# Residual additions of a one-layer hybrid encoder moved from GpSimd into accumulating DMAs on a copy of x in DRAM

## The chip, the core and the metric

The kernel runs on one core of a Trainium2 chip. The metric is the device time of one execution in microseconds; lower is better. Everything is fp32: each matrix product is made of three matmuls on a high and a low half (`fp32r`), which keeps fp32 accuracy. The engines' names are those of the profile: PE (TensorE), DVE (VectorE), ACT (ScalarE), POOL (GpSimd), and SP (SyncE), which does nothing here but issue DMAs.

## The reference, cut to what matters

`x_prompt` has 2048 rows and `x_sample` 128 rows (8 x 16) of 1024 columns. In tiles of 128 rows that makes 17 tiles, 0 to 15 for the prompt and 16 for the sample. The layer is

```python
h = rms_norm(x, norm_g[0])
z = h @ w_in                                   # 3592 columns: q, k, v of attention and of the mLSTM, gates
...                                            # chunk-band attention, mLSTM
mix = jnp.concatenate([att, mlstm_out], axis=-1) @ w_out
x = x + rms_norm(mix, norm_g[1])
ffn, new_buf = conv_ffn(rms_norm(x, norm_g[2]), conv_buf, w_up, w_conv, b_conv, w_down)
x = x + rms_norm(ffn, norm_g[3])
```

The change concerns the two lines `x = x + rms_norm(...)`.

## The kernel before, in words

The kernel is one function, `hymba_step`, with many nested helpers and generators. The source gives instructions and their data dependences; the order in which each engine's queue holds them is set when the program is built, by a scheduler that estimates when each instruction could start (`schedule_with_timeline_sim=True`). Only where the source says `tc.keep_in_program_order` does an instruction stay where it was written. At run time each engine works through its queue strictly in order, and an instruction that must wait holds up all that stand behind it. That is so for DMAs as well: SP and POOL issue them in the order of their queues, and an issue that has to wait (for a buffer, for data) blocks the later ones.

The stages, in order of time:

1. **Projection w_in and mixing** (0 to about 1050 us). The rows of x are loaded tile by tile (`xr`, L224), normed (square on ACT L228, `rsqrt` on POOL L87 and L93, scaling on DVE L231), transposed on PE (`hT_pt`, L76), and split into high and low halves (ACT L210, DVE L211). With these, PE works through 14 groups of 256 columns of w_in, `va0` first (`va`, L104 to L106), then `qk0`. The weights of a group come in two loads into a single raw buffer (`wi_raw`, L1213), so the second load is issued only when the first has been split by ACT L1219 and DVE L1220. In `va0` the nine tiles 0 to 7 and 16 are normed while PE uses the first of them; tiles 1, 4, 7 and 16 share one buffer for their rows, tiles 2 and 5 another, tiles 0, 3 and 6 two more, so the load of tile 4 waits for the transposes of tile 1, that of tile 7 for those of tile 4, that of tile 16 for those of tile 7. Attention and the mLSTM run between the groups.
2. **Projection w_out** (about 1050 to 1330 us; `project`, L974 on). Per tile t: the mixed rows `mr` are normed, transposed and split (`mt`), PE multiplies them by w_out in two halves (`wo`), DVE copies the result into the first 1024 columns of a buffer `mx` (L1026), its squares are summed, and DVE scales it by the norm (L1038). The second 1024 columns of `mx` are named `xr`: SP loads x into them at the start of the tile (L1016), POOL adds the two (L1039), SP stores the sum to `x2d[t]` in DRAM (L1040). `mx` has two buffers of the tag `wl`, which the weights of the next stage (`wul`, L1310) take over at the end.
3. **ConvFFN in three blocks** of 6, 6 and 5 tiles (about 1330 to 2776 us). Each block has an up stage (22 steps f, with `conv` per step: POOL copies two columns between `halo` and the tiles `uu`, `ug`, L1494 and L1499, and DVE L1503 and L1504 need them) and a down stage. The block's rows come from `x2d` (`x2r`, L1079). The result of a block's down stage goes to DRAM (`f0d`, `f1d`), and is finished during the up stage of the next block, in the generators `later` and `delayed`: per tile and half, SP loads the half `v` and the half `x` of `x2d[t]` (L1427, L1428), DVE scales `v` by the norm (L1431), POOL adds `x` (L1432) and issues the store to the output (L1433). There are 24 such units, 12 in block 1 and 12 in block 2. The last block finishes itself at the end (`load_rest`, `finish`), also from `x2d`.

Of the kernel before, what the change touches and what calls it, by code (L numbers as in the profile page):

```python
# [13 lines left out]
ALU = mybir.AluOpType  # L14
# [4 lines left out]
D = 1024  # L19
# [30 lines left out]
def hymba_step(ctx: ExitStack, tc: tile.TileContext, I: dict, O: dict):  # L50
    nc = tc.nc
# [8 lines left out]
    def ps_mm(name):  # L60
        return psum.tile([P, 512], F32, tag="mm", name=name)
# [7 lines left out]
    def spare_tile(name):  # L69
        return spare.tile([P, 512], F32, tag="k", name=name)  # L70

    def dt_(shape, name):
        return dram.tile(shape, F32, tag=name, name=name)
# [12 lines left out]
    def mean_square(ms, ssq, n, eps=EPS):  # L86
        nc.gpsimd.tensor_scalar(ms, ssq, 1.0 / n, eps, op0=ALU.mult, op1=ALU.add)  # L87

    def rsqrt_mean(ssq, n, name, eps=EPS):
        ms = small.tile([P, 1], F32, tag="ms", name=name + "_ms")  # L90
        mean_square(ms, ssq, n, eps)
        rs = small.tile([P, 1], F32, tag="rs", name=name + "_rs")
        nc.gpsimd.tensor_tensor(rs, ms, nhalf[:, 0:1], op=ALU.pow)  # L93
        return rs

    def norm_row(i):
        t = const.tile([P, D], F32, tag="grow", name=f"norm_row{i}")
        nc.sync.dma_start(t, I["norm_g"][i:i + 1, :].broadcast_to([P, D]))
        return t


    def mm3(out, ah, al, bh, bl, start, stop, onto=False):

        nc.tensor.matmul(out, ah, bh, start=start, stop=False, skip_group_check=onto)  # L104
        nc.tensor.matmul(out, ah, bl, start=False, stop=False, skip_group_check=onto)  # L105
        nc.tensor.matmul(out, al, bh, start=False, stop=stop, skip_group_check=onto)  # L106
# [21 lines left out]
    x2d = [dt_([P, D], f"x2d{t}") for t in range(17)]  # L128

    def x_src(t):  # L130
        return I["x_sample"] if t == SAMPLE else I["x_prompt"][t * P:(t + 1) * P, :]
# [69 lines left out]
    def rows_to_T(hrow, chunk, j, name, bank):  # L201
        w = 4 if bank is not ps_big else KT
        for q in range(KT // w):
            pt = bank(f"{name}_pt{q}")
            for k in range(w):
                transpose(pt[:, k * P:(k + 1) * P], hrow[:, (w * q + k) * P:(w * q + k + 1) * P])
            ptv = pt.rearrange("p (k t) -> p k t", k=w)
            hv = chunk[:, 0, w * q:w * q + w, j * P:(j + 1) * P]
            lv = chunk[:, 1, w * q:w * q + w, j * P:(j + 1) * P]
            nc.scalar.copy(hv, ptv)  # L210
            nc.vector.tensor_tensor(lv, ptv, hv, op=ALU.subtract)  # L211
# [4 lines left out]
    def rows_tile(tag, shape, name, dtype=F32):  # L216
        if tag == "xr":
            return rows.tile(shape, dtype, tag="xr", name=name, bufs=2)
        return pa.tile(shape, dtype, tag=tag, name=name, bufs=1)
# [750 lines left out]
    def drain():  # L970
        while any([p_.step() for p_ in pipes]):
            pass

    def project(tiles):  # L974

        ss = [SimpleNamespace(t=t) for t in tiles]

        def load(s):
            t = s.t
            if t == 8:  # L980
                drain()
                open_ffn()
            s.m = rows_tile("xr", [P, D], f"mr{t}")
            if t == SAMPLE:
                for b in range(DB):
                    own = bass.AP(atts[b].tensor, atts[b].offset, [[512, DS], [DS * 512 + DA, HA], [1, DA]])
                    nc.sync.dma_start(s.m[b * DS:(b + 1) * DS, 0:512].rearrange("p (h d) -> p h d", h=HA), own)
                nc.sync.dma_start(s.m[:, 512:D], mixs)
            else:
                nc.sync.dma_start(s.m, mixd[t // 4][:, t % 4, :])  # L990

        def norm(s):
            mt = wpool.tile([P, 2112], F32R, tag="wh", name=f"mt{s.t}", bufs=2)
            ssq = small.tile([P, 1], F32, tag="ssq", name=f"assq{s.t}")
            nc.scalar.activation(mt[:, :512], s.m[:, :512], AF.Square, accum_out=ssq)
            rs = rsqrt_mean(ssq, 512, f"att{s.t}")
            nc.vector.tensor_scalar(s.m[:, :512], s.m[:, :512], rs, None, op0=ALU.mult)
            s.mt = mt[:, :2 * D].rearrange("p (a k n) -> p a k n", a=2, k=KT)

        def turn_rows(s):  # L1000
            rows_to_T(s.m, s.mt, 0, f"mT{s.t}", ps_mm if s.t < 8 else ps_big)

        load(ss[0])
        norm(ss[0])
        yield 0.0, 0.3
        turn_rows(ss[0])
        load(ss[1])
        yield 0.9, 1.2
        for n_, s in enumerate(ss):
            t = s.t  # L1010
            nxt = ss[n_ + 1] if n_ + 1 < len(ss) else None
            if nxt:
                norm(nxt)
            mx = wpool.tile([P, 2112], F32, tag="wl", name=f"mx{t}", bufs=2)
            m, xr = mx[:, 0:D], mx[:, D:2 * D]
            nc.sync.dma_start(xr, x_src(t))  # L1016
            for hf in range(2):
                c = slice(hf * 512, hf * 512 + 512)
                acc = ps_mm(f"wo{t}_{hf}")
                for k in range(KT):  # L1020
                    mm3(acc, s.mt[:, 0, k, :], s.mt[:, 1, k, :], wo[k][0][:, c], wo[k][1][:, c],
                        start=(k == 0), stop=(k == KT - 1))
                    if k % 4 == 3:
                        yield 2.6, 0.5
                ssq = small.tile([P, 1], F32, tag="wssq", name=f"wssq{t}_{hf}")
                nc.vector.tensor_copy(m[:, c], acc)  # L1026
                idle = m[:, 512:D] if hf == 0 else s.mt[:, 0, 0:4, :].rearrange("p k n -> p (k n)")
                nc.scalar.activation(idle, m[:, c], AF.Square, accum_out=ssq)
                if hf == 0:
                    ssa = ssq  # L1030
                    mean_square(ssa, ssq, D)
                    if nxt:
                        turn_rows(nxt)
                        if n_ + 2 < len(ss):
                            load(ss[n_ + 2])
                        yield 0.9, 1.2
            rs = rsqrt_mean(ssq, D, f"n1_{t}", ssa)
            nc.vector.scalar_tensor_tensor(m, m, rs, g1[0], op0=ALU.mult, op1=ALU.mult)  # L1038
            nc.gpsimd.tensor_tensor(xr, m, xr, op=ALU.add)  # L1039
            nc.sync.dma_start(x2d[t], xr)  # L1040

# [5 lines left out]
    def open_ffn():  # L1049

        p1.close()
        ffn.p3 = ctx.enter_context(tc.tile_pool(name="p3", bufs=2, reuse_waits="tile"))
        ffn.halo = ffn.p3.tile([P, 44, 2], F32, tag="halo", name="halo", bufs=1)
        nc.vector.memset(ffn.halo, 0.0)
        ffn.g2 = ffn.p3.tile([P, D], F32, tag="g2", name="g2", bufs=1)
        nc.sync.dma_start(ffn.g2, I["norm_g"][2:3, :].broadcast_to([P, D]))
        pipes[:] = [Pipe(h2_units(0, lead=6)), Pipe(iter([]))]
# [187 lines left out]
    for n_, (half, gi) in enumerate(seq):  # L1245
# [22 lines left out]
        if n_ == len(seq) - 1:  # L1268
            out = project([0, 1, 2, 3, 4, 5, 6, 7, SAMPLE, 8, 9, 10, 11, 12, 13, 14, 15])
            split = w_out_steps()  # L1270
            next(split)
            next(out)
# [128 lines left out]
    def out_rows(t):  # L1401
        return O["y_sample"] if t == SAMPLE else O["y_prompt"][t * P:(t + 1) * P, :]
# [20 lines left out]
    def later(t, rs):  # L1423

        def unit(half):
            v, x, c = spare_tile(f"f{half}{t}"), spare_tile(f"x{half}{t}"), half * 512
            tc.keep_in_program_order(nc.sync.dma_start(v, (f0d, f1d)[half][t]))  # L1427
            tc.keep_in_program_order(nc.sync.dma_start(x, x2d[t][:, c:c + 512]))  # L1428
            yield 0.0, 0.0
            tc.keep_in_program_order(  # L1430
                nc.vector.scalar_tensor_tensor(v, v, rs, g3[:, c:c + 512], op0=ALU.mult, op1=ALU.mult))  # L1431
            nc.gpsimd.tensor_tensor(v, v, x, op=ALU.add)  # L1432
            nc.gpsimd.dma_start(out_rows(t)[:, c:c + 512], v)  # L1433
            yield 0.0, 1.0

        return [unit(half) for half in range(2)]

    def delayed(units):

        for u in units:  # L1440
            next(u)
            yield
            next(u)

    ph.close()
    p4 = ffn.p4 = ctx.enter_context(tc.tile_pool(name="p4", bufs=1, side="right", reuse_waits="tile"))
# [3 lines left out]
    g3 = norm_row(3)  # L1450
# [15 lines left out]
    for b, tiles in enumerate(FBLOCKS):  # L1466
# [124 lines left out]
        for fi, f in enumerate(ORDERS[b]):  # L1591
# [12 lines left out]
            e, c = ec[:, 0:512], ec[:, 512:1024]  # L1604
# [120 lines left out]
        for dh in range(2):  # L1725
# [59 lines left out]
            for j in order:  # L1785
                if dh == 0:
                    half, ssq = out[j]
# [3 lines left out]
                else:  # L1791
                    half, ssq = out[j]
# [3 lines left out]
                    rs = p3.tile([P, 1], F32, tag=f"drs{j}", name=f"drs{tiles[j]}", bufs=2)  # L1796
# [104 lines left out]
```

## Time and profile before

| | |
|---|---|
| median of 3 runs | 2776.57 us (2775.95 to 2780.12) |
| the profiled execution: its own time | 2778.06 us |
| the profiled execution: its span | 2776.4 us, granted PE clock 0.997 |
| busy share of the span: PE, DVE, ACT, POOL | 97%, 70%, 51%, 22% |
| DMA | 522.15 MB, mean 188 GB/s |

A row of the timeline shows start, duration, engine, line, operation, out<-in, shapes, count, and in brackets how long the engine sat idle before it and what ended that. "SPq" and "POOLq" rows of DMA are the issue alone: the transfer lands later, which a waiting engine shows as "<-DMA". Busy shares in the view of stretches are us of each engine in the stretch, the granted clock, the mean busy share of the 16 DMA engines and the GB/s that they moved.

### The profile page before, as it was taken

How to read it: one execution, taken by the hardware profiler on the slowest of the kernel's cores; microseconds unless marked ns; L12 is line 12 of the kernel's file. 1: busy time of each engine (PE TensorE's matmuls, PEld its weight loads, DVE VectorE, ACT ScalarE, POOL GpSimd, SP SyncE). 2: the span in 40 equal slices, each digit the busy share in tenths (PEclk: the TensorE clock that was granted, in tenths of full speed). 3: DMA queues.
4: the chain of work that ended last, by engine and by line, in shares of the span. 5: the costliest groups of instructions: out<-in, count | busy, mean ns of one | idle time of the engine just before them, and what ended most of it. 6: DMA issues, size and time to landing. Idle time of an engine off the chain costs nothing.

```text
span 2776.4 us, 47521 instructions
## 1 busy us (share of the span) xinstructions
PE 2704.6 (97%) x16488; PEld 2530.5 (91%) x16488; DVE 1938.4 (70%) x3563; ACT 1420.4 (51%) x2879; POOL 610.1 (22%) x1177
## 2 busy tenths in 40 slices
PE   8999999999999999999999999999999999999998
PEld 7899999998899998878999998789999778999886
DVE  5344455646546668766999987668998866999744
ACT  4355555634356666543545455445455665555542
POOL 1000010211100002344433322123442102344100
PEclk9999999999999999999999999999999999999999
DMA  5544355556554456345645559866775767776655
GB/s 183 157 118 137 103 164 169 161 151 210 161 182 142 140 165 196 107 166 197 227 157 181 170 192 326 299 223 198 232 220 168 251 218 233 219 238 202 193 184 180
DMA packets 317664, 522.15 MB, mean 188 GB/s; under 512 B 58210, under 2 KB 154302, under 8 KB 317294
## 3 DMA queue, kind: packets, MB, share of 16 engines
q1 hardware_dynamic: 249246, 394.21, 46.3%
q0 software_dynamic: 23248, 79.51, 7.5%
q10 hardware_dynamic: 44928, 45.37, 5.0%
q8 instruction: 130, 2.13, 0.3%
q14 instruction: 112, 0.92, 0.1%
HBM read 377.38 MB, written 144.72 MB: 188 GB/s over the span
## 4 chain that ended last, share of the span: by engine, by line
PE 53%; DVE 3%; issue 2%; DMA 2%; ACT 1%; POOL 1%; DVEq 0%; POOLq 0%; SPq 0%; ACTq 0%
PE uec L104 6%; PE uec L105 6%; PE uec L106 6%; PE dn L106 3%; PE dn L104 3%; PE dn L105 3%; PE ua L106 3%; PE ua L105 3%; PE ua L104 3%; PE dnm L106 2%; PE dnm L105 2%; PE dnm L104 2%; PE wo L106 2%; PE wo L104 2%; PE wo L105 2%
## 5 line engine op out<-in xcount | busy, mean ns | idle before, releaser
L104 PE MATMUL uec<-B,wuh 128*128 128x384 f32 (+1 forms) x720 | 235.4, 328 | 3.2 <-DVE uu L1632 1.7
L105 PE MATMUL uec<-B,wuh 128*128 128x384 f32 (+1 forms) x720 | 235.1, 327 | 0.0
L106 PE MATMUL uec<-B,wul 128*128 128x384 f32 (+1 forms) x720 | 233.5, 327 | 0.0
L1309 ACT CAST wuh<-wu 128x512 fp32r<-128x512 f32 x255 | 141.7, 618 | 114.3 <-PE uec L105 106.3
L1310 DVE TENSOR_TENSOR wul<-wu,wuh 128x512 fp32r<-128x512 f32 x255 | 168.3, 695 | 4.1 <-DMA x2d<-mx 2.9
L405 DVE CUSTOM_DVE_ANT_0 tmp<-s,nb 128x640 f32<-128x640 f32 (+4 forms) x128 | 94.3, 737 | 95.1 <-PE s L395 93.4
L104 PE MATMUL vo<-wi_h,hT 128*128 128x256 f32 x544 | 155.2, 285 | 0.6 <-DVE mt L211 0.6
L106 PE MATMUL vo<-wi_h,hT 128*128 128x256 f32 x544 | 155.6, 286 | 0.0
L105 PE MATMUL vo<-wi_l,hT 128*128 128x256 f32 x544 | 154.8, 285 | 0.0
L1310 DVE TENSOR_TENSOR gl<-gr,gh 128x768 fp32r<-128x768 f32 (+3 forms) x92 | 73.9, 812 | 98.9 <-ACT gh L1309 91.1
L104 PEld LDWEIGHTS uec<-B,wuh 128*128 128x128 f32 x720 | 135.0, 188 | 5.3 <-DVE uu L1632 2.3
L1309 ACT CAST gh<-gr 128x768 fp32r<-128x768 f32 (+3 forms) x92 | 65.0, 719 | 143.8 <-PE dn L105 110.3
L104 PE MATMUL qk<-hT,wi_h 128*128 128x384 f32 (+1 forms) x384 | 129.1, 336 | 7.1 <-ACT qk_st L236 5.3
L105 PEld LDWEIGHTS uec<-B,wuh 128*128 128x128 f32 x720 | 135.2, 188 | 0.2
L106 PEld LDWEIGHTS uec<-B,wul 128*128 128x128 f32 x720 | 135.1, 188 | 0.0
L418 DVE TENSOR_TENSOR ptl<-pt,pth 128x640 fp32r<-128x640 f32 (+4 forms) x128 | 93.6, 737 | 58.4 <-ACT pth L417 57.5
L406 ACT ACTIVATE tmp<-tmp,mn 128x640 f32<-128x640 f32 (+4 forms) x128 | 97.6, 762 | 65.0 <-DVE mn L405 62.4
L105 PE MATMUL qk<-hT,wi_h 128*128 128x384 f32 (+1 forms) x384 | 128.0, 333 | 0.0
L105 PE MATMUL qb<-hT,wi_h 128*128 128x384 f32 (+1 forms) x384 | 127.8, 333 | 0.0
L106 PE MATMUL qk<-hT,wi_l 128*128 128x384 f32 (+1 forms) x384 | 127.5, 332 | 0.0
L106 PE MATMUL qb<-hT,wi_l 128*128 128x384 f32 (+1 forms) x384 | 127.2, 331 | 0.0
L104 PE MATMUL qb<-hT,wi_h 128*128 128x384 f32 (+1 forms) x384 | 127.1, 331 | 0.0
(447 smaller groups left out, 9335.1 us busy)
## 6 DMA issues: line engine op xcount, KB each, us to landing
wu<-in_w_up SPq DMA_DIRECT2D x220, 256.0 KB, 4.3
wu<-wsd SPq DMA_DIRECT2D x176, 256.0 KB, 3.8
wdr<-in_w_down SPq DMA_DIRECT2D x121, 256.0 KB, 5.6
wi_raw<-in_w_in SPq DMA_DIRECT2D x52, 512.0 KB, 4.1
wsd<-ws POOLq DMA_DIRECT2D x88, 256.0 KB, 3.5
gr<-gd SPq DMA_DIRECT2D x39, 384.0 KB, 6.7
kraw<-kTd SPq DMA_DIRECT2D x112, 128.0 KB, 3.3
gr<-gd SPq DMA_DIRECT2D x39, 320.0 KB, 4.6
```

The source lines that it names most:

```text
L104: nc.tensor.matmul(out, ah, bh, start=start, stop=False, skip_group_check=onto)
L105: nc.tensor.matmul(out, ah, bl, start=False, stop=False, skip_group_check=onto)
L106: nc.tensor.matmul(out, al, bh, start=False, stop=stop, skip_group_check=onto)
L405: nc.vector.tensor_tensor_reduce(o_, s_, b_, 1.0, 3e38, ALU.add, ALU.min, accum_out=mn)
L406: nc.scalar.activation(tmp[:, :n], tmp[:, :n], AF.Exp, bias=mn, scale=-1.0, accum_out=rsum[:, i % 4, hh:hh + 1])
L418: nc.vector.tensor_tensor(s.ptl[:, sl, qc], ptv, s.pth[:, sl, qc], op=ALU.subtract)
L1309: nc.scalar.copy(h, r)
L1310: nc.vector.tensor_tensor(l, r, h, op=ALU.subtract)
```

## The change

Before the w_out sum exists, x is copied whole from the input to `x2d[t]` by a DMA from DRAM to DRAM (17 of 512 KB, on SP). The normed result of w_out is then added to it by an accumulating DMA that POOL issues, in place of POOL's addition and SP's store. In the delayed units the normed half is likewise accumulated onto `x2d[t]` in DRAM, and a second DMA copies the half row from `x2d[t]` to the output; the loads of x go. `delayed` is written so that this copy follows one unit later.

```diff
             mx = wpool.tile([P, 2112], F32, tag="wl", name=f"mx{t}", bufs=2)
-            m, xr = mx[:, 0:D], mx[:, D:2 * D]
-            nc.sync.dma_start(xr, x_src(t))
+            m = mx[:, 0:D]
+            nc.sync.dma_start(x2d[t], x_src(t))
...
             nc.vector.scalar_tensor_tensor(m, m, rs, g1[0], op0=ALU.mult, op1=ALU.mult)
-            nc.gpsimd.tensor_tensor(xr, m, xr, op=ALU.add)
-            nc.sync.dma_start(x2d[t], xr)
+            nc.gpsimd.dma_start(x2d[t], m, accum_op=ALU.add)
...
         def unit(half):
-            v, x, c = spare_tile(f"f{half}{t}"), spare_tile(f"x{half}{t}"), half * 512
+            v, c = spare_tile(f"f{half}{t}"), slice(half * 512, half * 512 + 512)
             tc.keep_in_program_order(nc.sync.dma_start(v, (f0d, f1d)[half][t]))
-            tc.keep_in_program_order(nc.sync.dma_start(x, x2d[t][:, c:c + 512]))
             yield 0.0, 0.0
             tc.keep_in_program_order(
-                nc.vector.scalar_tensor_tensor(v, v, rs, g3[:, c:c + 512], op0=ALU.mult, op1=ALU.mult))
-            nc.gpsimd.tensor_tensor(v, v, x, op=ALU.add)
-            nc.gpsimd.dma_start(out_rows(t)[:, c:c + 512], v)
-            yield 0.0, 1.0
+                nc.vector.scalar_tensor_tensor(v, v, rs, g3[:, c], op0=ALU.mult, op1=ALU.mult))
+            nc.gpsimd.dma_start(x2d[t][:, c], v, accum_op=ALU.add)
+            yield 0.0, 0.7
+            nc.gpsimd.dma_start(out_rows(t)[:, c], x2d[t][:, c])
+            yield 0.0, 0.0
...
     def delayed(units):
-        for u in units:
-            next(u)
+        for u, old in zip(units + [iter([])], [iter([])] + units):
+            next(u, None)
             yield
-            next(u)
+            next(u, None)
+            next(old, None)
```

The multiset of instructions on PE, DVE and ACT is the same in both programs. What moves is shown at two places. (From L1016 on, lines of the changed kernel stand one lower than before.)

The first place is the very start of SP's queue, which holds DMA issues alone: `wi0_raw1` is the second half of the weights of group `va0`, `wi1_raw0` the first of group `qk0`, `xr4` the rows of tile 4. Before, these rows stand there:

```order
L503 DMA hgm0_0_4088<-in_g_mlstm 128x128
L1213 DMA wi0_raw1_379<-in_w_in0 128x1056
L224 DMA xr6_632<-in_x_prompt 128x1024
L310 DMA ext_952<-reln_405 8x384
L311 DMA ext_952<-relf_953 8x383
L224 DMA xr4_529<-in_x_prompt 128x1024
L1213 DMA wi1_raw0_422<-in_w_in1 128x1024
L224 DMA xr5_580<-in_x_prompt 128x1024
L224 DMA xr7_681<-in_x_prompt 128x1024
L1213 DMA wi1_raw1_527<-in_w_in1 128x1024
```

In the changed program the queue goes on from the same `hgm0` like this:

```order
L503 DMA hgm0_0_4088<-in_g_mlstm 128x128
L1016 DMA x2d0_295<-in_x_prompt 16x8192
L1016 DMA x2d1_296<-in_x_prompt 16x8192
L1016 DMA x2d2_297<-in_x_prompt 16x8192
L1016 DMA x2d3_298<-in_x_prompt 16x8192
L1212 DMA wi0_raw1_379<-in_w_in0 128x1056
L224 DMA xr6_632<-in_x_prompt 128x1024
L310 DMA ext_952<-reln_405 8x384
L311 DMA ext_952<-relf_953 8x383
L1016 DMA x2d4_299<-in_x_prompt 16x8192
L1016 DMA x2d5_300<-in_x_prompt 16x8192
L1016 DMA x2d6_301<-in_x_prompt 16x8192
```

After `x2d7` come the load of tile 4 (`xr4`), four more copies, the load of tile 5, and then the last five copies, ahead of the weights of `qk0`:

```order
L224 DMA xr5_580<-in_x_prompt 128x1024
L1016 DMA x2d11_306<-in_x_prompt 16x8192
L1016 DMA x2d12_307<-in_x_prompt 16x8192
L1016 DMA x2d13_308<-in_x_prompt 16x8192
L1016 DMA x2d14_309<-in_x_prompt 16x8192
L1016 DMA x2d15_310<-in_x_prompt 16x8192
L1212 DMA wi1_raw0_422<-in_w_in1 128x1024
L224 DMA xr7_681<-in_x_prompt 128x1024
L224 DMA xr8_6732<-in_x_prompt 128x1024
L1212 DMA wi1_raw1_527<-in_w_in1 128x1024
L1212 DMA wi2_raw0_842<-in_w_in1 128x1024
L224 DMA xr16_730<-in_x_sample 128x1024
```

So the 17 copies, which wait for no data, do not stand at the w_out stage where they are written, but among the first loads of the program: 4 ahead of `wi0_raw1`, 8 ahead of the rows of tile 4, 12 ahead of those of tile 5, all 17 ahead of `wi1_raw0`.

The second place is POOL's queue in the up stage of block 1, at the second half of tile 2 (`f12`) and the first of tile 3 (`f03`). Before, POOL adds, then issues the store to the output:

```order
L1432 TENSOR_TENSOR f12_22027<-f12_22027,x12_22028 128x512
L1433 DMA out_y_prompt<-f12_22027 128x512
L1494 COPY uu1_3_22411<-halo_15180 128x2
L1573 DMA ad1_A11_251<-y1_2_0_22154 128x384
L1573 DMA ad1_S3_256<-s3_1_2_22313 128x384
L1494 COPY ug1_3_22427<-halo_15180 128x2
L1499 COPY halo_15180<-ug1_13_22259 128x2
L1432 TENSOR_TENSOR f03_22182<-f03_22182,x03_22183 128x512
```

In the changed program the same stretch of POOL's queue reads:

```order
L1430 DMA x2d2_297<-f12_22007 128x512
L1432 DMA out_y_prompt<-x2d2_297 128x512
L1494 COPY uu1_3_22385<-halo_15173 128x2
L1573 DMA ad1_A11_251<-y1_2_0_22132 128x384
L1573 DMA ad1_S3_256<-s3_1_2_22289 128x384
L1494 COPY ug1_3_22401<-halo_15173 128x2
L1499 COPY halo_15173<-ug1_13_22235 128x2
L1430 DMA x2d3_298<-f03_22160 128x512
```

The copy to the output (L1432) stands directly behind, or one or two small copies behind, the accumulating DMA (L1430) of its own half, not a unit later as `delayed` has it; it waits until that DMA has landed, and the copies of `uu` and `halo` stand behind it.

## The prediction

> **What bounds the kernel now.** I read the page's busy times first, then stretches of the span, then the timeline at the three places where the change moves something. The page's line of busy times:
>
> ```profile
> PE 2704.6 (97%) x16488; PEld 2530.5 (91%) x16488; DVE 1938.4 (70%) x3563; ACT 1420.4 (51%) x2879; POOL 610.1 (22%) x1177
> ```
>
> PE is busy for 2704.6 of 2776.4 us. So at most 71.8 us could ever be gained without touching PE's work, and whatever makes PE idle longer is paid in full. The stretches (length, then busy us of PE, PEld, DVE, ACT, POOL, then clock, DMA share, GB/s) for the start and for the stages behind it:
>
> ```profile
> 0.00:5.00 5.00, 0.00 (x0) 0.00 (x0) 0.72 (x6) 2.12 (x2) 1.93 (x15) 1.00 0.62 177
> 5.00:10.00 5.00, 1.54 (x7) 1.54 (x8) 2.04 (x3) 1.64 (x5) 0.74 (x2) 1.00 0.98 349
> 10.00:15.00 5.00, 2.96 (x13) 2.25 (x12) 4.23 (x7) 4.47 (x8) 2.33 (x6) 1.00 0.98 331
> 15.00:20.00 5.00, 5.00 (x39) 5.00 (x38) 4.26 (x5) 2.97 (x6) 0.15 (x1) 1.00 0.48 154
> 65.00:70.00 5.00, 5.00 (x31) 4.69 (x31) 3.46 (x21) 0.25 (x1) 0.00 (x0) 1.00 0.98 287
> ...
> 1050.00:1200.00 150.00, 146.60 (x865) 126.38 (x864) 112.95 (x223) 85.20 (x218) 45.68 (x68) 1.00 0.42 134
> 1200.00:1345.00 145.00, 141.15 (x694) 117.84 (x693) 104.68 (x112) 62.47 (x120) 64.52 (x80) 1.00 0.62 213
> 1345.00:1750.00 405.00, 400.65 (x2169) 379.25 (x2168) 358.24 (x541) 207.78 (x339) 129.37 (x221) 1.00 0.62 206
> 1750.00:2230.00 480.00, 473.81 (x2514) 443.61 (x2515) 394.45 (x582) 245.76 (x419) 152.96 (x256) 1.00 0.71 229
> ```
>
> The first 15 us are the one place where the DMA engines are full (0.98) and PE is not. In the w_out stage (1050 to 1345) PE is idle for 295 - 146.60 - 141.15 = 7.25 us in all, in the ConvFFN blocks for about 1% of the time. So the additions that the change removes are beside a full PE, and what they can give back is capped by these few us. What it puts at the start is not beside anything.
>
> **The start: 17 copies ahead of the first loads.** SP's issues in the first 37 us, and the engines that wait for what they load:
>
> ```profile
> 10.60 0.33 SPq L1213 DMA_DIRECT2D wi_raw<-in_w_in  x1
> 15.28 0.36 SPq L224 DMA_DIRECT2D xr<-in_x_prompt  x1
> 18.15 0.36 SPq L1213 DMA_DIRECT2D wi_raw<-in_w_in  x1
> 25.09 0.86 SPq L1213 DMA_DIRECT2D wi_raw<-in_w_in  x1
> 34.51 0.33 SPq L1213 DMA_DIRECT2D wi_raw<-in_w_in  x1
> 36.35 0.33 SPq L224 DMA_DIRECT2D xr<-in_x_sample  x1
> ```
>
> ```profile
> 14.50 1.17 ACT L1219 CAST wi_h<-wi_raw 128x528 fp32r<-128x528 f32 x2 [0.53 <-DMA wi_raw<-in_w_in]
> 18.61 1.06 ACT L228 ACTIVATE hT<-xr 128x1024 fp32r<-128x1024 f32 x1 [2.03 <-DMA xr<-in_x_prompt]
> 22.24 1.14 ACT L1219 CAST wi_h<-wi_raw 128x512 fp32r<-128x512 f32 x2 [1.30 <-DMA wi_raw<-in_w_in]
> 24.39 0.68 DVE L1220 TENSOR_TENSOR wi_l<-wi_raw,wi_h 128x512 fp32r<-128x512 f32 x1
> 23.18 0.66 PE L76 MATMUL hT_pt<-ident,xr 128*128 128x128 f32 x4
> 46.01 1.03 PE L76 MATMUL hT_pt<-ident,xr 128*128 128x128 f32 x8
> ```
>
> These give four durations. A load of 512 KB on free DMA engines takes 18.61 - 15.28 = 3.33 us from issue to use. From the rows' landing to the tile's transposes it is 23.18 - 18.61 = 4.57 us. The raw weights, landed at 22.24, are used up by 25.07 (24.39 + 0.68), 2.83 us later, and the next load of the single raw buffer goes out at 25.09. From one raw load's issue to the next it was 25.09 - 18.15 = 6.94 us.
>
> A copy moves 512 KB. At the 349 GB/s of the full stretch it holds the DMA engines for 1.50 us, so 17 hold them for 25.5 us. No copy from DRAM to DRAM of this size stands in the trace; the bounds are below. Loads that SP issues behind a copy come behind it, as the loads of the first 15 us come one after another. Now the chain in the changed queue:
>
> - `wi0_raw1` is behind 4 copies: landed at 14.50 + 6 = 20.5. PE can by then do only the first halves of tiles 0 and 1, so it stalls already here.
> - Tile 4 is behind 8 copies, tile 5 behind 12; `wi1_raw0` behind all 17. Before, the DMA engines were idle for about 2.6 us of 15 to 20 (share 0.48); that gap closes. So `wi1_raw0` lands at 22.24 - 2.6 + 25.5 = 45.1.
> - Its second half is issued when the raw buffer is used up, 45.1 + 2.83 = 47.9; the next raw load 6.94 later, at 54.9; the rows of tile 16 stand behind that in SP's queue, 0.45 later (two issues), at 55.3. They are in use at 55.3 + 3.3 = 58.6, and transposed on PE at 58.6 + 4.6 = 63.2.
>
> Before, PE came to the transposes of tile 16 at 46.01, and everything else of `qk0` is behind them in its queue. So PE is late by 63.2 - 46.0 = **17 us**, and nothing gives that back: from there on it is 97% busy, and its later waits hang on data that are late with it.
>
> The price of a copy from the other side: the stretch 65 to 70, in which the kernel's own DRAM-to-DRAM transfers (`relrow<-ext`) run, shows 0.98 and 287 GB/s, 1.83 us per copy, 31 us for 17. The slowest kind of large packet on the page, with others of this view:
>
> ```profile
> q8 instruction: 130, 2.13, 0.3%
> ...
> wsd<-ws POOLq DMA_DIRECT2D x88, 256.0 KB, 3.5
> wtd<-fold POOLq DMA_DIRECT2D x44, 256.0 KB, 6.3
> x2d<-mx SPq DMA_DIRECT2D x17, 512.0 KB, 2.7
> out_y_prompt<-f POOLq DMA_DIRECT2D x24, 256.0 KB, 3.8
> ```
>
> 2.13 MB in 0.3% of 16 x 2776.4 us is 16 GB/s per engine, 256 GB/s for 16, or 2.05 us per copy and 34.8 us for 17. I take 1.50, since that row is of 512 KB loads at the same place. The upper end adds 9.3 us, to 26 us. The lower end, where only the wait for tile 5 counts and the last chain is hidden, is tile 5 behind 12 copies: 18 us, less the 2.6 idle and the 3.1 of tile 3's 24 matmuls (39 take 5 us in 15 to 20), which now stand ahead of that wait, 12 us.
>
> **The w_out stage.** Out go 17 additions, 17 loads and 17 stores of 512 KB; in come 17 accumulating DMAs.
>
> ```profile
> L1039 POOL TENSOR_TENSOR mx<-mx 128x1024 f32<-128x1024 f32 x17 | 41.0, 2415 | 2.5 <-DVE mx L1038 2.5
> L1432 POOL TENSOR_TENSOR f<-f,x 128x512 f32<-128x512 f32 x24 | 50.6, 2108 | 24.3 <-DVE f L1431 24.2
> ...
> L997 DVE TENSOR_SCALAR mr<-mr,att_rs x17: 476/2605/2621, 1011.3 to 1301.0; 128x512 f32<-128x512 f32 x17
> ...
> 1317.89 0.69 DVE L1310 TENSOR_TENSOR wul<-wu,wuh 128x512 fp32r<-128x512 f32 x1 [2.85 <-DMA x2d<-mx]
> 1312.70 2.42 POOL L1039 TENSOR_TENSOR mx<-mx 128x1024 f32<-128x1024 f32 x1 [1.40 <-DVE mx L1038]
> ```
>
> POOL saves 41 us. DVE's L997 takes 0.48 us at best and 2.6 as a rule, as long as the addition beside it: some 17 x 2.1 = 36 us of DVE come free. Little of that reaches PE, which idles only 7.25 us here; I take 2 us gained. The Trainium skill ("SBUF — State Buffer", Who interferes with whom) says that DVE and GpSimd share a port pair and that a DVE `tensor_scalar` in a two-port mode and GpSimd block each other for the whole instruction. The row of L997 agrees. By this rule the change should also speed DVE; it moves my sum by no more than the cap above.
>
> At the stage's end `wul` waits for the last `mx` to leave: from 1312.6, when DVE is done with it, to 1317.9, 5.3 us (2.42 addition, then the store's 2.7). An accumulating DMA is in no row. The nearest are POOL's stores of 256 KB, 3.5 to 6.3 us; with 0.55 for the issue, 4.1 to 6.9, so -1.2 to +1.6 us. I take 0. If it took twice the slowest, 12.6 us, it would be +8 here, once.
>
> **The delayed units.** Per unit POOL loses an addition of 2.1 us, but now waits for its accumulating DMA before the copy to the output, with the `halo` and `uu` copies queued behind. What can wait there, and who needs it:
>
> ```profile
> 1914.07 0.56 POOL L1433 DMA_DIRECT2D out_y_prompt<-f  x1 [0.89 <-POOL f L1432]
> 1914.78 0.19 POOL L1494 COPY uu<-halo 128x2 f32<-128x2 f32 x1
> ...
> 1920.61 1.02 DVE L1503 SCALAR_TENSOR_TENSOR y<-uu,wcv,y 128x768 f32<-128x768 f32 x1 [0.64 <-ACT y L1502]
> 1923.42 1.14 ACT L1309 CAST wuh<-wu 128x512 fp32r<-128x512 f32 x2 [2.92 <-PE uec L105]
> ```
>
> `uu` has 5.6 us until DVE reads it, and the weights are split 2.9 us before PE could take them. At a landing of 3.8 us (the store `out_y_prompt`) the queue is 3.8 - 2.1 = 1.7 us later: hidden. I take 0.
>
> **Sum.** +17 - 2 = +15 us. The profiled execution took 2778.06 us, 1.5 over the median of 2776.57. On the median that is 2791.6; I say **2792**. Its own range is 2776.6 + 12 - 7 = 2782, with all of the w_out stage's idle gained, to 2776.6 + 26 + 5 = 2808, with nothing gained there and part of the 8 us lost.
>
> **The rivals.**
>
> - *The copies are hidden*: they give way to the loads, or PE makes up for them in `qk0`. For it: the DMA engines are idle soon after 15 us. Against it: the raw buffer and the shared row buffers make each load wait for the one before. 2775 to 2782.
> - *Faster*: the copies hide, and POOL's and DVE's freed time closes most of the 7.25 us of the w_out stage: 2776.6 - 7 = 2770. It needs both.
> - *A copy costs twice*, as it both reads and writes DRAM: 1 MB at 349 GB/s, 3.0 us, 51 us for 17, 25.5 more than above: 2817. Against it: 287 GB/s at 65 to 70, not half of 349. The Trainium skill ("DMA: Bandwidth & Descriptors", Where 436 GB/s comes from) names about 358 GB/s as a core's share of HBM; if both directions count, 1 MB would take 2.9 us, an estimate that puts the time at about the same 2817. No run here shows such a pure copy.
> - *The accumulating DMAs are slow and POOL's queue chokes*: a landing of 12.6 us holds POOL 10.5 us longer per unit. Beyond the 5.6 of `uu` and the 2.9 of the weights 2.0 us are left for PE, times 24 is 48 us: 2840. It decides from a landing of about 10 us.
>
> **Chances.** Forecast 0.64, hidden 0.12, faster 0.04, double price 0.08, choked POOL 0.08, something slower between these 0.04. A measurement of this kernel can tell about 0.2%, 5.6 us, from no change. Faster by more: 0.04. Within: 0.12. Slower: 0.64 + 0.08 + 0.08 + 0.04 = 0.84. The range 2778 to 2820 takes in the forecast, the double price and half of the hidden case, 0.78.
>
> **What would show it.** In the changed profile `va0` would have a stall before the second half of the weights (ACT's cast at about 20.5 instead of 14.5), the DMA share would stay near 0.98 until about 45, and the transposes of tile 16 would start near 63 instead of 46; 15 to 17 us of PE's additional idle would lie in the first 65 us, and the stages behind would keep their lengths to within 5 us. L997 would fall to about 0.5 us. I am wrong if the cast stays at 14.5, if PE's idle grows in the up stages of blocks 1 and 2, or if a copy takes far from 1.5 us.

## The result, and the profile after

| | before | after |
|---|---|---|
| median of the runs | 2776.26 us (4 runs, 2773.72 to 2780.12) | 2802.19 us (4 runs, 2797.33 to 2803.97) |
| profiled execution, own time and span | 2778.06, 2776.4 us | 2801.57, 2799.9 us |
| mean granted clock | 0.997 | 0.993 |

The ratio is 1.0089, 95% interval 1.0075 to 1.0104: the changed kernel is 25.9 us slower. The forecast was 2792, slower, with 2778 to 2820 as its range.

The busy times of the changed kernel's page:

```profile
PE 2716.6 (97%) x16488; PEld 2540.1 (91%) x16488; DVE 1889.6 (67%) x3563; ACT 1420.8 (51%) x2879; POOL 561.8 (20%) x1177
```

DVE lost about 49 us of work and POOL about 48. PE has the same 16488 matmuls, and its busy time grew by 12 us. So the work that the change removed did come free, and the kernel is slower all the same. Where it lost shows in stretches of one piece of work. First the kernel before, from 15 us to the transposes of tile 16 (46.01), and the 54 us behind them (length, busy us of PE, PEld, DVE, ACT, POOL, then clock, DMA share, GB/s):

```profile
15.00:46.01 31.01, 29.52 (x241) 28.93 (x240) 21.34 (x29) 17.04 (x30) 4.68 (x10) 1.00 0.52 168
46.01:100.00 53.99, 48.05 (x284) 45.39 (x283) 21.09 (x82) 16.12 (x36) 0.58 (x4) 1.00 0.51 147
```

The same pieces of the changed kernel, where these transposes start at 72.41, and three later stages, shifted by PE's delay at their ends:

```profile
15.00:72.41 57.41, 37.11 (x239) 35.24 (x239) 22.03 (x30) 18.43 (x31) 4.65 (x10) 0.85 0.71 240
72.41:126.40 53.99, 51.28 (x285) 48.44 (x286) 20.83 (x82) 14.97 (x32) 0.58 (x4) 0.94 0.48 143
...
1076.40:1371.40 295.00, 288.20 (x1554) 244.73 (x1553) 184.75 (x332) 147.09 (x337) 83.55 (x147) 0.99 0.54 140
1371.40:1776.50 405.10, 401.32 (x2172) 379.71 (x2171) 359.65 (x543) 207.98 (x339) 129.10 (x221) 1.00 0.62 208
1776.50:2257.00 480.50, 476.61 (x2516) 446.31 (x2517) 384.67 (x582) 245.61 (x418) 134.83 (x256) 0.99 0.72 228
```

The first piece is 57.41 - 31.01 = 26.4 us longer, and what lies behind it keeps its length: 53.99 beside 53.99, the w_out stage 295.00 beside 295, the ConvFFN blocks 405.10 beside 405 and 480.50 beside 480. PE's delay is 26.4 us from 100 to 400 us and 26.7 at 1600. (It falls to 24 from 2500 on, but behind 2000 it falls by 2 us or more in every other profile of this document too, so that is the profile of before.) The whole loss is in the first 72 us. In the two pieces together PE idles 20.30 + 2.71 us instead of 1.49 + 5.94, 15.6 more, and is busy 88.39 instead of 77.57, 10.8 more for the same matmuls, at a granted clock of 0.85 and 0.94.

SP's issues there (start, us over the row, engine, line, transfer, count):

```profile
9.72 3.25 SPq L1016 DMA_DIRECT2D x2d<-in_x_prompt  x4
13.09 0.51 SPq L1212 DMA_DIRECT2D wi_raw<-in_w_in  x1
...
15.24 4.21 SPq L1016 DMA_DIRECT2D x2d<-in_x_prompt  x4
21.72 0.37 SPq L224 DMA_DIRECT2D xr<-in_x_prompt  x1
...
27.89 6.07 SPq L1016 DMA_DIRECT2D x2d<-in_x_prompt  x5
35.41 0.33 SPq L1212 DMA_DIRECT2D wi_raw<-in_w_in  x1
...
55.45 6.04 SPq L1212 DMA_DIRECT2D wi_raw<-in_w_in  x2
62.47 0.33 SPq L224 DMA_DIRECT2D xr<-in_x_sample  x1
```

And ACT, which casts the raw weights, squares the rows and issues the stores of the `v` rows:

```profile
21.76 1.17 ACT L1218 CAST wi_h<-wi_raw 128x528 fp32r<-128x528 f32 x2
27.41 0.37 ACT L236 COPY va_st<-va 128x256 f32<-128x256 f32 x1 [4.48 <-PE va L106]
36.55 0.35 ACTq L287 DMA_DIRECT2D vd<-va_st  x1
36.94 0.37 ACT L236 COPY va_st<-va 128x256 f32<-128x256 f32 x1 [9.16 <-DMA x2d<-in_x_prompt]
...
52.87 1.14 ACT L1218 CAST wi_h<-wi_raw 128x512 fp32r<-128x512 f32 x2
...
68.98 1.06 ACT L228 ACTIVATE hT<-xr 128x1024 fp32r<-128x1024 f32 x1 [4.65 <-DMA xr<-in_x_sample]
```

The copies stand where the prediction put them. `wi0_raw1` is cast at 21.76 instead of 14.50, `wi1_raw0` at 52.87 instead of 22.24. One row was not foreseen: ACT had its first `va_st` ready at 27.78, but issued the store only at 36.55. Nothing else ran on ACT for 9 us, and the profile names an x copy as the reason, a transfer that ACT has nothing to do with.

The semaphores in the trace tell why. The transfers that SP and ACT issue count their landing on eight counters, which the two engines use in turn, and one is issued only when the one that used its counter before has landed. ACT's store waits on the counter of the copy that SP issued at 24.73. The last count of that copy comes at 36.48, and the store goes out at 36.55.

So besides what SP queues behind the copies, there is a second way from the copies to PE: ACT waits for a copy to land, and its squares and casts stand behind that store.

The row of DVE's L997, and three of the transfers that came in (KB each, median us from issue to landing):

```profile
L997 DVE TENSOR_SCALAR mr<-mr,att_rs x17: 477/487/489, 1037.9 to 1329.5; 128x512 f32<-128x512 f32 x17
```

```profile
x2d<-mx POOLq DMA_DIRECT2D x17, 512.0 KB, 5.5
...
x2d<-in_x_prompt SPq DMA_DIRECT2D x16, 512.0 KB, 9.7
x2d<-f POOLq DMA_DIRECT2D x24, 256.0 KB, 5.4
```

L997 fell from 2.6 us to 0.49, as forecast, and gave PE nothing: PE was busy 288.2 of 295 us in the w_out stage, 287.75 before.

### The profile page after: what moved, and what is told of

It reads as the page before. It is cut to its first block, busy times and chain, and to the rows that moved or that the text cites. A ratio compares the mean times of both kernels' runs of the same rounds, so it can differ in the third digit from the quotient of the medians.

```text
span 2799.9 us, 47434 instructions
## 1 busy us (share of the span) xinstructions
PE 2716.6 (97%) x16488; PEld 2540.1 (91%) x16488; DVE 1889.6 (67%) x3563; ACT 1420.8 (51%) x2879; POOL 561.8 (20%) x1177
## 4 chain that ended last, share of the span: by engine, by line
PE 53%; DVE 3%; DMA 2%; issue 1%; ACT 1%; POOL 0%; SPq 0%; DVEq 0%; POOLq 0%; ACTq 0%
PE uec L104 6%; PE uec L105 6%; PE uec L106 6%; PE dn L106 3%; PE dn L105 3%; PE dn L104 3%; PE ua L106 3%; PE ua L105 3%; PE ua L104 3%; PE dnm L106 2%; PE dnm L105 2%; PE dnm L104 2%; PE wo L104 2%; PE wo L106 2%; PE wo L105 2%; PE ub L105 1%
```

## The experiments

The theory, START: all of the loss comes from the copies at the start. Its rival, ACCUMULATE: the accumulating transfers and the waits for them cost a good part. Later theories are told where they came up. All ratios are against the kernel before on the same chip. PE's delay is the start of the same matmul in two profiles.

### The copies late

```
-            nc.sync.dma_start(x2d[t], x_src(t))
+            tc.keep_in_program_order(nc.sync.dma_start(x2d[t], x_src(t)))
```

> The change as it is, but the 17 copies keep their place in the program, so that they are issued in the w_out stage and not at the start. Theory START (all of the loss comes from the copies that stand ahead of the first loads): the tile-16 transposes are back at 46 us, and the time is 2772 to 2779 us, that of the kernel before. Rival ACCUMULATE (the accumulating transfers, the waits of POOL for them and the longer way through DRAM cost a good part): the start is as in the kernel before, but the time stays 10 us or more above it, 2786 to 2802 us, with the loss in the w_out stage or in the ConvFFN blocks.

Measured: 2793.64 us, ratio 1.0066 (1.0052 to 1.0081). START's time missed by far, and ACCUMULATE's was hit. The start is free again (the tile-16 transposes at 45.63), but PE loses time at two later places, some 9 us at the end of the w_out stage and some 11 us in the down part of the first ConvFFN block. For the first the rows tell the chain. SP, POOL, DVE and PE:

```profile
1297.45 1.26 SPq L1016 DMA_DIRECT2D x2d<-in_x_prompt  x2
1298.81 13.49 SPq L1320 DMA_DIRECT2D wu<-in_w_up  x7
```

```profile
1309.45 0.69 DVE L1325 TENSOR_TENSOR ws<-wu,wu 128x512 f32<-128x512 f32 x1 [2.64 <-DMA wu<-in_w_up]
1310.06 0.68 DVE L1026 COPY mx<-wo 128x512 f32<-128x512 f32 x1
...
1326.67 0.69 DVE L1309 TENSOR_TENSOR wul<-wu,wuh 128x512 fp32r<-128x512 f32 x1 [7.67 <-DMA x2d<-mx]
```

```profile
1315.99 0.94 POOL L1039 DMA_DIRECT2D x2d<-mx  x1 [0.25 <-DVE mx L1038]
```

```profile
1327.42 0.69 PE L106 MATMUL ua<-B,wul 128*128 128x384 f32 x1 [7.68 <-DVE wul L1309]
```

Two copies stand ahead of the first weight rows of the ConvFFN. These land late, DVE's `ws` addition waits for them, `mx` is evacuated behind that, its accumulate is issued at 1315.99 and lands about 10.7 us later, and only then is the buffer free for `wul`. PE stands for 7.68 us. Both seem to be needed, copies at a bad place and an accumulate that is slower than the store that it replaced: in the changed kernel itself, with the same accumulates and no copies here, PE waits for `wul` 0.5 us (1.6 before). Late copies beside plain stores were not tried. Since here too the copies stand ahead of loads that PE needs soon, this run could not decide between the theories. For the second place the profile shows that loads of `gr` come later in SP's queue; the cause was not separated and stays open.

### The copies alone

```
             nc.sync.dma_start(xr, x_src(t))
+            nc.sync.dma_start(xcd[t], x_src(t))
```

> The kernel before, with nothing of the change but 17 copies of x, to a scratch tensor in DRAM that nobody reads, written at the same place in the code and left free to move. Output and all additions are those of the kernel before. START: they move to the start of SP's queue as in the changed kernel, the tile-16 transposes come at 72 us instead of 46, and the time is 2799 to 2806 us. ACCUMULATE: copies that hardly matter by themselves, under 10 us, 2776 to 2786 us.

Measured: 2801.37 us, ratio 1.0096 (1.0082 to 1.011), as START expected. The transposes come at the time of the changed kernel (72.41), and ACT waits for a copy as there (9.16):

```profile
72.59 1.97 PE L76 MATMUL hT_pt<-ident,xr 128*128 128x128 f32 x8 [3.11 <-DVE xr L232]
```

```profile
35.94 0.37 ACT L237 COPY va_st<-va 128x256 f32<-128x256 f32 x1 [8.02 <-DMA xcd<-in_x_prompt]
```

17 copies that nobody reads, with every addition left as it was, cost what the whole change costs.

### The v stores from another queue

```
-                nc.scalar.dma_start(dst[s][:, 0 if s == 4 else t % 4, :], stage[:, :256])
+                first = nc.gpsimd if name == "va0_0" else nc.scalar
+                first.dma_start(dst[s][:, 0 if s == 4 else t % 4, :], stage[:, :256])
```

> The changed kernel, with the eight stores of the first group's v rows (vd<-va_st, 128 KB each) issued by POOL instead of ACT. Theory LANE (ACT stood still from 27.8 to 36.6 us because its store had to wait for the landing of an x copy that SP had issued, and ACT's squares and casts stood behind that store): that idle time of ACT goes, the second copy va_st<-va comes before 33 us instead of 36.94, the cast of wi1_raw0 at 46 to 48 us instead of 52.9, the tile-16 transposes at 64 to 68 instead of 72.4, and the time is 2793 to 2798 us. Rival BYTES (the 9 us are only another sight of full DMA engines, and something else that needs the same bytes is late at the same time): the transposes stay at 70 us or later, the time at 2799 to 2804 us.

Measured: 2799.18 us, ratio 1.0087 (1.0073 to 1.0101). LANE's time is missed, BYTES' is hit, and the ratio cannot be told from that of the changed kernel (1.0089). The trace can be read more finely:

```profile
28.79 0.37 ACT L236 COPY va_st<-va 128x256 f32<-128x256 f32 x1 [0.67 <-PE va L106]
...
48.06 1.14 ACT L1219 CAST wi_h<-wi_raw 128x512 fp32r<-128x512 f32 x2 [0.87 <-DMA wi_raw<-in_w_in]
```

```profile
66.86 1.09 PE L76 MATMUL hT_pt<-ident,xr 128*128 128x128 f32 x8 [1.40 <-DVE xr L231]
```

All three places are where LANE put them, or within 0.1 us of it: the second copy at 28.79 (36.94 in the changed kernel), the cast at 48.06 (52.87), the transposes at 66.86 (72.41). PE's delay from 100 to 400 us is 22.1 us, where the three profiles with ACT's wait (the changed kernel, the copies alone, and the run with rows of 4 KB below) have 26.4 to 27.4. So in the traces the shared counters are worth 4 to 5 us of the 26. The times are too close to show it: the interval of the ratio overlaps those of the changed kernel (1.0075 to 1.0104) and of the copies alone, and this profile is of one of the two fastest of the six executions (2796.15 us).

### The delayed units alone

The kernel before with `later` and `delayed` of the changed one:

```
-            nc.gpsimd.tensor_tensor(v, v, x, op=ALU.add)
-            nc.gpsimd.dma_start(out_rows(t)[:, c:c + 512], v)
+            nc.gpsimd.dma_start(x2d[t][:, c], v, accum_op=ALU.add)
+            yield 0.0, 0.7
+            nc.gpsimd.dma_start(out_rows(t)[:, c], x2d[t][:, c])
```

> The kernel before with only the second half of the change: the delayed norms add onto x2 in DRAM by an accumulating transfer, and a copy brings the row to the output. The w_out stage is that of the kernel before, so there are no early copies. START: 2772 to 2778 us, no difference or up to 3 us gained in the third ConvFFN block, where the changed kernel's delay fell from 26.6 to 24.2 us. ACCUMULATE: 5 us or more slower, 2781 us or above, as POOL waits 41 us in all for its accumulates to land.

Measured: 2771.81 us, ratio 0.9989 (0.9979 to 0.9999). That is 0.2 us below START's range, and ACCUMULATE's 2781 is out. POOL waits 41 us in all for accumulates to land in the changed kernel, and with these waits in it the run is no slower. Whether the units gain a little stays open: PE's lead of 3 to 4 us in this profile is there before the first unit runs, at code that is the same in both.

### The copies in the middle

```
-            nc.sync.dma_start(x2d[t], x_src(t))
...
+        for c in range(0 + 4 * (n_ - 12), min(17, 0 + 4 * (n_ - 12 + 1))) if n_ >= 12 else ():
+            tc.keep_in_program_order(nc.sync.dma_start(x2d[c], x_src(c)))
```

> The change as it is, but the 17 copies are issued four at a time with five of the projection groups of the middle (the 13th to the 17th of 28), hundreds of us after the start and hundreds before the w_out stage ends; the accumulating transfers stay. Theory START: the copies have room there, and the accumulates cost nothing; 2770 to 2780 us, the time of the kernel before, with the first weight rows of the ConvFFN (wul) waited for by PE at most 2 us. Rival ACCUMULATE (what was lost in the run with late copies, 9 us in the wait for wul at the end of the w_out stage and 10 us in the down part of the first ConvFFN block, belongs to the accumulates and had only been covered by the late start): 2786 to 2798 us, with PE idle again at these two places.

Measured: 2779.16 us, ratio 1.0015 (1.0003 to 1.0027), within START's bounds. The copies are issued between 526 and 704 us. The transposes of tile 16 are back, PE waits 0.8 us for `wul`, and the same 295 us of the w_out stage, with all 17 accumulates in them, have PE as busy as before:

```profile
46.38 1.04 PE L76 MATMUL hT_pt<-ident,xr 128*128 128x128 f32 x8
```

```profile
1050.00:1345.00 295.00, 287.98 (x1550) 243.76 (x1550) 183.28 (x332) 146.74 (x338) 83.83 (x147) 0.99 0.54 141
```

This decides what the run with late copies could not. With the copies where SP's queue has room, the whole change, copies included, costs 0.8 to 7.5 us by the interval and gains nothing, though 34 us of DVE and 26 of POOL are gone from this stage.

### Eight copies early

The run before, with the first eight copies left free; they move to the places that they have in the changed kernel, and the loop of the run before issues the other nine. In the w_out stage:

```
+            if t < 8:
+                nc.sync.dma_start(x2d[t], x_src(t))
```

> As the run before in this list, but the first 8 copies are left free and move to the start, where they stand at the same two places of SP's queue as in the changed kernel (4 ahead of wi0_raw1, 8 ahead of tile 4); the other 9 are issued in the middle. Theory QUEUE+LANE (the copies delay what is queued behind them, and the last nine do most of it, as they alone stand ahead of wi1_raw0 and ahead of ACT's first store): wi0_raw1 is as late as in the changed kernel (its cast at 21 to 22 us), ACT has no wait of 9 us, the tile-16 transposes come at 49 to 54 us, and the time is 3 to 9 us above the kernel before, 2778 to 2784. Rival BYTES (every copy costs its share of 26 us): 12 us above it, 2786 to 2790.

Measured: 2789.51 us, ratio 1.0043 (1.0029 to 1.0056). QUEUE+LANE's time is missed and BYTES' is hit. In the trace the answer is mixed. ACT has no wait for a copy, and the cast of `wi0_raw1` is at 21.85, both as QUEUE+LANE has it; the transposes come at 55.31, later than its 49 to 54:

```profile
55.31 1.09 PE L76 MATMUL hT_pt<-ident,xr 128*128 128x128 f32 x8 [2.64 <-DVE xr L231]
```

That is 9.3 us late, where an equal share of 26.4 would be 12.4. More is lost later: the medians differ by 12.8 us, and in this profile PE's delay is 14 us at 1680 and 11 at 2690. In the run before, with copies in the middle alone, it lies mostly between 0 and 5 us and is 4 at 1680, so the nine in the middle probably have a part in this time. Eight copies cost about 9 us at the start, the other nine about 17: not in proportion, but less far from it than I expected.

### The copies on POOL's queue

```
-            nc.sync.dma_start(x2d[t], x_src(t))
+            nc.gpsimd.dma_start(x2d[t], x_src(t))
```

> The changed kernel with the 17 copies issued on POOL's queue instead of SP's. They are at its start too, ahead of the norm steps of tile 0, but no load of SP stands behind one. Theory QUEUE+LANE: what is behind the copies in their new queue is late instead; from the ninth on each copy waits for an earlier one to land, and n_rs of tile 0 stands behind 16 of them, so the first transposes come some 14 us late and the time is 12 to 22 us above the kernel before, 2787 to 2797. Rival BYTES (full DMA engines are the cost, whoever issues): 24 to 29 us above it, 2799 to 2804, as in the changed kernel. If only SP's own queue mattered it would be under 5 us above.

Measured: 2813.09 us, ratio 1.0131 (1.0114 to 1.0148). All three expectations are too low. The copies are issued from 2.54 us on. DVE then waits for a small load that SP issued at 8.44 us, and behind that for the second half of the weights, which ACT casts when it lands; the scaling of the rows, without which PE can't begin, stands behind both:

```profile
39.52 0.23 DVE L504 TENSOR_SCALAR hgm<-hgm 128x128 f32<-128x128 f32 x1 [22.19 <-DMA hgm<-in_g_mlstm]
```

```profile
40.86 1.16 ACT L1218 CAST wi_h<-wi_raw 128x528 fp32r<-128x528 f32 x2 [6.31 <-DMA wi_raw<-in_w_in]
```

```profile
44.10 1.11 PE L76 MATMUL hT_pt<-ident,xr 128*128 128x128 f32 x4 [44.10 <-DVE xr L231]
```

The small load, 64 KB, is in use 31 us after its issue, in the kernel before after 5.7 (issued at 8.57, used at 14.3). SP's earlier loads stand ahead of it in both; no copy is ahead of it in its queue. The new theory, TURNS: the DMA engines take the two queues in turn row by row, and a copy's rows have 32 KB, a load's 4.

### Copies with rows of 4 KB, on SP's queue and on POOL's

```
-    x2d = [dt_([P, D], f"x2d{t}") for t in range(17)]
+    x2d = [dt_([P, D + 16], f"x2d{t}")[:, 0:D] for t in range(17)]
```

> The changed kernel, with x2 in DRAM given 16 unused floats behind each row, so that a copy is 128 rows of 4 KB instead of 16 of 32 KB. Bytes, number of transfers and the order on every engine are those of the changed kernel. Theory QUEUE+LANE (the copies cost by standing ahead of other transfers in one queue, whatever their rows): 2796 to 2804 us, and a start like that of the changed kernel. Rival ROWS (it is the 32 KB rows that make the copies dear, alone or beside other queues' rows): 8 us or more less, 2792 us or below.

> The run before it in which POOL issues the copies, which began PE's work at 44.1 us and lost 36 us, with the same 4 KB rows. Theory TURNS (two queues take turns row by row, so that SP's loads of 4 KB rows got a small share beside rows of 32 KB: a load issued at 3.5 us landed at 33.4 us): with rows of one size SP's loads get about half, the last load that the start needs lands by 25 us instead of 39.5, PE begins at 30 to 35 us, and the time is 10 to 14 us less, 2799 to 2804. Rival: the size of the rows does not matter, PE begins at 42 us or later and the time stays at 2810 to 2816 us.

Measured on SP's queue: 2801.36 us, ratio 1.0095 (1.008 to 1.0109). PE's delay from 100 to 400 us is 26.4 us, that of the changed kernel. In one queue the size of the rows makes no difference, as QUEUE+LANE has it.

Measured on POOL's queue: 2801.56 us, ratio 1.01 (1.0086 to 1.0115) instead of 1.0131 with rows of 32 KB. The time and PE's begin are where TURNS put them. (The two runs were on different chips; against the kernel before on its own chip the gain is about 9 us, not 10 to 14.) The small load is in use at 22.87, and the second half of the weights lands at 25.9, just behind TURNS' 25. But then PE's begin hangs on something else, on POOL's `n_rs` of tile 0, which stands behind all 17 copies in POOL's queue; QUEUE+LANE of the run before had named it. DVE and PE:

```profile
22.87 0.23 DVE L504 TENSOR_SCALAR hgm<-hgm 128x128 f32<-128x128 f32 x1 [11.42 <-DMA hgm<-in_g_mlstm]
...
31.94 1.28 DVE L231 SCALAR_TENSOR_TENSOR xr<-xr,n_rs,norm_row 128x1024 f32<-128x1024 f32 x1 [4.05 <-POOL n_rs L93]
```

```profile
33.28 1.97 PE L76 MATMUL hT_pt<-ident,xr 128*128 128x128 f32 x8 [33.28 <-DVE xr L231]
```

The queues from 8 to 24 us (packets, MB, share of the engines; q0 is POOL's, q1 SP's and ACT's), first with rows of 32 KB, then with 4 KB:

```profile
q0 software_dynamic: 283, 4.72, 82.0%
q1 hardware_dynamic: 291, 1.01, 18.7%
```

```profile
q0 software_dynamic: 1098, 4.02, 65.3%
q1 hardware_dynamic: 1013, 2.05, 34.6%
```

In both, the two queues move nearly the same number of packets, and the bytes go as the mean size of a packet: 16.7 KB beside 3.5 in the first run, 3.7 beside 2.0 in the second. (The means are below the size of the rows because the profile counts small packets too: on POOL's queue of the first run 144 rows of 32 KB and 139 packets of 4 bytes.) The Trainium skill ("DMA: Bandwidth & Descriptors", Queues, rings and completion order) says that a DMA engine goes round the queues that have work and takes a whole packet from each. The equal counts agree with that, but the page puts 9 to 17 descriptors into a typical packet, and here a packet of the profile is a single row or four bytes.

This last run also serves as a control for the clock. PE's delay in it is 25.3 us from 200 to 400, with this line of its page:

```profile
PE 2706.2 (97%) x16488; PEld 2529.2 (90%) x16488; DVE 1888.3 (67%) x3563; ACT 1421.5 (51%) x2879; POOL 578.8 (21%) x1194
```

Its PE is busy 1.6 us longer than before, not 12. So slow matmuls are not needed for a loss of this size. In the changed kernel, whose stalls come in pieces, the granted clock falls to 0.85 up to 72.41, and 10.8 us of the 26.4 are slower matmuls. That PE would mostly have waited in that time anyway is likely, but not shown: how much a full clock would give back was not tried.

## Why the prediction was right, and where its size was off

- **What bounds the kernel.** Right. The 49 us that DVE and the 48 us that POOL shed bought nothing, since PE was the bound there, and PE lost only at the start, where it waits for loads. The copies alone show it.
- **Where the copies stand and what a copy costs.** Right. The order is the one shown ahead, and a copy held the DMA engines about as long as the forecast 1.50 us. In the run in which POOL issues the copies, nothing else is on its queue in the first 45 us (packets, MB, share of 16 engines):

```profile
q0 software_dynamic: 544, 8.91, 55.1%
```

That is 24.8 us for 17 copies, 1.46 us each, and it settles the rival of the double price against it.

- **The chain to the transposes of tile 16.** Its steps were right and its size too small, 63.2 instead of 72.41, 17.2 us late instead of 26.4. Two terms were mis-sized.

  The first is the cast of `wi1_raw0`, forecast for 45.1, the time at which the load would land. In the changed kernel the last count of that load comes at 47.3, 2.2 us later, but ACT casts it only at 52.87, another 5.6 us later. The sum followed only what SP queues behind the copies and took ACT as free. It left out that ACT's store shares counters with SP's copies, so that ACT stands still from 27.8 to 36.55. In the run in which POOL issues the stores, the cast starts as the load lands, at 48.06.

  The second is the load of tile 16's rows, 6.5 us from issue to use instead of 3.33. Half of that was a misreading: 3.33 is from the load of tile 4, and the load of tile 16 itself had taken 41.34 - 36.35 = 5.0 us in the kernel before, as this row shows with the issue at 36.35:

```profile
41.34 1.06 ACT L228 ACTIVATE hT<-xr 128x1024 fp32r<-128x1024 f32 x1 [3.96 <-DMA xr<-in_x_sample]
```

In the changed kernel 15 of the load's 16 counts are there at 67.02, 4.6 us after its issue, the last at 68.90; why that one is late stays open. The other terms held: from the cast to the second raw load's issue 2.58 us (forecast 2.83), from there to the issue for tile 16 7.0 (7.4), from use to the transposes 3.4 (4.57). 2.2 + 5.6 - 0.25 - 0.4 + 3.2 - 1.1 = 9.25 us, against the 9.2 that were missing.
- **PE's idle time.** The forecast 15 to 17 us of additional idle were met, 15.6, but by luck. They were to be the whole delay, and the delay is 26.4: the other 10.8 us are matmuls at a lower granted clock, for which the sum had no term.
- **The upper bound of 26 us** was met, but by other terms than the dearer copy that it stood for; that is luck as well.
- **The w_out stage.** 2 us of gain forecast, none measured: PE is busy 288.20 of 295 us after and 287.75 before. `wul` costs PE 0.5 us in the changed kernel, within the bounds given. In the run with late copies an accumulate takes 10.7 us and PE waits 7.68, near the 8 that the sum named for a slow accumulate, but there another delay came first.
- **The delayed units.** 0 forecast; the run with them alone is at 0.9989 (0.9979 to 0.9999). An accumulate of 256 KB landed in 5.4 us (4.5 to 7.4), longer than the 3.8 taken, and still below the 10 us from which POOL's queue would have mattered.
- **The rivals.** The hidden copies are out by the copies alone, the faster case by the copies in the middle, the choked POOL by the delayed units.

## What to carry to other kernels

An operation that waits for nothing may be moved to the start of a queue by the scheduler, and the start is where the loads were the bound here; look for such an operation in the new order and hold it at a place where the DMA engines have room. Then follow its delay along every way on which others wait for it: its own queue, the counters that it shares with other engines' transfers, and the DMA engines, where a queue of large rows took the larger part. Work taken off an engine that the bound does not wait for was worth nothing here, 48 us of it on each of two engines.

## What the runs showed of the hardware that was not expected

- Two queues on full DMA engines moved equal numbers of packets, not of bytes: 283 beside 291 with 4.72 and 1.01 MB, 1098 beside 1013 with 4.02 and 2.05 MB. A load of 64 KB with other loads ahead of it was in use 31 us after its issue in the first case, 14 in the second (issued at 8.70, used at 22.87), 5.7 in the kernel before.
- A copy from DRAM to DRAM did not cost twice a load of its size: 512 KB held the DMA engines for 1.46 us in the run with the copies on POOL's queue. Rows of 32 KB or of 4 made no difference to the time of the kernel when one queue held copies and loads (2802.19 and 2801.36 us).
- Transfers issued by SP and by ACT wait for each other through the counters that they share: a store of 128 KB on ACT waited 8.8 us for a copy that SP had issued, and held up ACT's own work behind it.
- An accumulate of 512 KB into DRAM landed 5.5 us after its issue (up to 11.7), and its issue held POOL 0.92 us; SP's plain store of the same rows had landed in 2.7.
